# A hybrid decoder layer on one core: FFN up-projection by seven quarter products, with the down-projection as a stage of its own

## The chip, the cores and the metric

One core of one Trainium2 chip runs the whole program. The metric is the device time of one execution in microseconds; three runs of the kernel before and the profile of one execution are given.

## What is computed

A decoder layer for 1024 tokens and 16 meta tokens in front of them (1040 columns; the kernels keep tokens on the free axis and channels on the partitions, in blocks of 128). Two branches, a chunked retention and a differential attention, are projected, mixed by sigmoid gates and added to the residual stream h; a gated MLP with a causal depthwise convolution of width 3 follows. The part around the change:

```python
y   = retention_out @ w_ret_o * sigmoid(gr) + diff_out @ w_diff_o * sigmoid(gd)
h   = x + y @ w_out                                   # (1040, 1024)
u   = rmsnorm(h, norm2_w) @ w_up                      # (1040, 2 * 2816)
u   = causal_dwconv(u, conv_w, conv_b)                # per channel, 3 taps
a, b = split(u)
out = h + (silu(a) * b) @ w_down                      # rows of the meta tokens removed
```

Everything is float32 to the reference's precision.

## The kernel before

Each float32 operand of a product is split into a high and a low fp32r part, and a product is three matmuls, high x high, high x low and low x high (`mm3`, `bulk`). Weights arrive as blocks [128, 8, 128] in two halves of 256 KB (`load_w`, L221); ScalarE casts a half to the high part (L227) and GpSimd subtracts for the low part (L230). A single list, `self.stream`, sets the order of weights, and `next_w` keeps one block ahead; all loads go through SyncE's queue. Activations are split by `split`: a cast on ScalarE (L242) and a subtraction on VectorE or GpSimd (L247). Every matmul is issued by line L175 and has its own weight load.

The program runs in four phases. Phases 1 and 2 are the projections, both attention branches and ret_out, with projection products put between the steps of the attention (`blend`), and with work that waits for other engines put off by some units (`defer`). Phase 3 merges: for each of 8 output blocks of diff_o and of w_out, three column groups of 342 (`QG`), 24 matmuls each. While w_out runs, squares of h are summed (L1025 on ScalarE, L1026 on GpSimd), and h times `norm2_w` is split (`normed`); the row statistics are put off into the first FFN products, and their reciprocal root, spread over the partitions in `rb2`, is multiplied in when the up-projection leaves PSUM (L1079).

Phase 4 loops over 22 channel blocks f. For each, two up products (blocks f and 22 + f), 3 groups of 24 matmuls of 342 columns each; VectorE takes them out of PSUM (L1079), then runs the convolution (`conv`: one TS, L1086, and two STT, L1088, of 1024 columns), ScalarE the Silu (L1124), VectorE the product (L1125), and ScalarE and GpSimd split it. Between the up products stands the down product of an earlier pair of blocks (`down`): 8 output blocks, two halves of 512 columns, 6 matmuls each, added to h in SBUF from PSUM (L1103). h stays in SBUF, and the last down product stores it to the output (L1105).

The order on each engine is the order of the program's calls; the tile framework puts semaphores where an instruction needs another's result or a buffer that another still reads.

## Time and profile before

| | |
|---|---|
| three runs, us | 2614.42, 2614.18, 2611.49; median 2614.18 |
| profiled execution, first to last instruction | 2609.7 us (what lies around it isn't listed) |
| TensorE matmuls | 15444, busy 2520.9 us (97%) |
| VectorE, ScalarE, GpSimd busy | 1667.5, 898.4, 865.4 us |
| first diff_o product to the last matmul's end | 1678.2 to 2606 us |
| granted clock, mean | 0.989 of 2.4 GHz |

Busy times of an engine can hide which stretch is limited by what, so the table is to be read with the stretches below. Times of a matmul in the views are from its start to its modelled end, and overlap; the step from start to start is its price.

### The profile page before, as it was taken

How to read it: one execution, taken by the hardware profiler on the slowest of the kernel's cores; microseconds unless marked ns; L12 is line 12 of the kernel's file. 1: busy time of each engine (PE TensorE's matmuls, PEld its weight loads, DVE VectorE, ACT ScalarE, POOL GpSimd, SP SyncE). 2: the span in 40 equal slices, each digit the busy share in tenths (PEclk: the TensorE clock that was granted, in tenths of full speed). 3: DMA queues.
4: the chain of work that ended last, by engine and by line, in shares of the span. 5: the costliest groups of instructions: out<-in, count | busy, mean ns of one | idle time of the engine just before them, and what ended most of it. 6: DMA issues, size and time to landing. Idle time of an engine off the chain costs nothing.

```text
span 2609.7 us, 40439 instructions
## 1 busy us (share of the span) xinstructions
PE 2520.9 (97%) x15444; PEld 2420.4 (93%) x15444; DVE 1667.5 (64%) x3359; ACT 898.4 (34%) x1903; POOL 865.4 (33%) x644
## 2 busy tenths in 40 slices
PE   7899999999999999999999999999999999999999
PEld 6898999999999999999999898999999999999998
DVE  8687877657474756654677888452376555555555
ACT  3344434344252433433456654332321111111111
POOL 4433343313132222212333333443333333333332
PEclk8999999999999999999999999999999999999999
DMA  4121221222222121223343434523111111111112
GB/s 175 58 78 64 67 79 61 81 87 67 84 64 78 57 87 62 75 83 103 108 115 86 120 88 122 177 98 112 45 48 47 49 49 49 43 47 49 49 49 85
DMA packets 165777, 205.37 MB, mean 79 GB/s; under 512 B 25560, under 2 KB 108112, under 8 KB 165584
## 3 DMA queue, kind: packets, MB, share of 16 engines
q1 hardware_dynamic: 165440, 202.70, 24.4%
q8 instruction: 121, 1.98, 0.3%
q14 instruction: 72, 0.59, 0.1%
q10 hardware_dynamic: 144, 0.10, 0.0%
HBM read 160.20 MB, written 42.35 MB: 78 GB/s over the span
## 4 chain that ended last, share of the span: by engine, by line
PE 76%; DVE 15%; issue 4%; ACT 2%; DMA 2%; SPq 1%; POOL 0%; DVEq 0%; ACTq 0%; POOLq 0%
PE acc L175 43%; PE sc L175 27%; PE ot L175 3%; DVE b L567 3%; PE st L175 2%; DMA b<-d 1%; DVE b L499 1%; ACT b L609 1%; PE sc L625 1%; DVE b L602 1%; DVE al L247 1%; DVE b L501 1%; DVE sql L247 1%; DVE sh L498 1%; DVE b L521 1%
## 5 line engine op out<-in xcount | busy, mean ns | idle before, releaser
L175 PE MATMUL acc<-b,wh 128*128 128x342 f32 (+3 forms) x6076 | 1484.6, 327 | 30.7 <-DVE b L252 6.6
L175 PEld LDWEIGHTS acc<-b,wh 128*128 128x128 f32 x6076 | 1055.1, 190 | 46.3 <-DVE b L253 7.3
L175 PE MATMUL acc<-b,wl 128*128 128x342 f32 (+3 forms) x3038 | 987.2, 325 | 0.3 <-POOL wl L230 0.3
L230 POOL TENSOR_TENSOR wl<-wr,wh 128x512 fp32r<-128x512 f32 x370 | 514.1, 1408 | 1114.2 <-ACT wh L227 1103.8
L175 PE MATMUL sc<-b,wh 128*128 128x342 f32 (+2 forms) x2452 | 616.2, 334 | 0.0
L175 PEld LDWEIGHTS acc<-b,wl 128*128 128x128 f32 x3038 | 577.0, 190 | 5.7 <-POOL wl L230 0.6
L175 PEld LDWEIGHTS sc<-b,wh 128*128 128x128 f32 x2452 | 432.1, 189 | 20.9
L227 ACT CAST wh<-wr 128x512 fp32r<-128x512 f32 x370 | 214.6, 618 | 574.2 <-issue 286.3
L175 PE MATMUL sc<-b,wl 128*128 128x342 f32 (+2 forms) x1226 | 410.6, 335 | 0.8 <-POOL wl L230 0.8
L247 POOL TENSOR_TENSOR b<-b,b 128x512 fp32r<-128x512 f32 (+2 forms) x90 | 147.9, 1644 | 317.2 <-ACT b L242 275.4
L175 PEld LDWEIGHTS sc<-b,wl 128*128 128x128 f32 x1226 | 231.8, 189 | 11.4 <-POOL wl L230 1.3
L242 ACT CAST b<-b 128x512 fp32r<-128x512 f32 (+2 forms) x135 | 99.9, 745 | 233.0 <-DVE b L1125 146.2
L609 ACT ACTIVATE b<-b,sm 128x272 f32<-128x272 f32 (+7 forms) x128 | 100.9, 789 | 227.0 <-DVE sm L608 174.6
L534 DVE TENSOR_TENSOR ev<-acc,b 128x342 f32<-128x342 f32 (+1 forms) x144 | 74.0, 514 | 132.8 <-PE acc L175 115.8
L1088 DVE SCALAR_TENSOR_TENSOR b<-b,cols,b 128x1024 f32<-128x1024 f32 x88 | 148.8, 1691 | 2.3
L602 DVE CUSTOM_DVE_ANT_0 b<-sc,consts 128x144 f32<-128x144 f32 (+6 forms) x224 | 105.9, 503 | 42.7 <-PE sc L175 42.1
L1079 DVE TENSOR_TENSOR b<-sc,b 128x342 f32<-128x342 f32 x84 | 42.5, 511 | 137.3 <-PE sc L175 137.3
L247 DVE TENSOR_TENSOR al<-sc,ah 128x512 fp32r<-128x512 f32 (+2 forms) x144 | 77.5, 539 | 56.8 <-ACT ah L242 55.4
L1103 DVE TENSOR_TENSOR b<-b,sc 128x512 f32<-128x512 f32 x117 | 78.6, 682 | 48.9 <-PE sc L175 48.9
L242 ACT CAST ah<-sc 128x512 fp32r<-128x512 f32 (+2 forms) x144 | 67.3, 468 | 122.3 <-PE sc L625 94.5
L500 POOL TENSOR_TENSOR sh<-sh,b 128x346 f32<-128x346 f32 (+1 forms) x48 | 47.7, 994 | 153.4 <-DVE sh L498 125.5
L567 DVE TENSOR_TENSOR b<-b,b 64x346 fp32r<-64x346 f32 (+1 forms) x96 | 89.4, 931 | 3.7 <-ACT b L566 0.7
(230 smaller groups left out, 2849.6 us busy)
## 6 DMA issues: line engine op xcount, KB each, us to landing
wr<-w_in SPq DMA_DIRECT2D x176, 256.0 KB
wr<-w_up SPq DMA_DIRECT2D x88, 256.0 KB
d<-ev SPq DMA_DIRECT2D x120, 171.0 KB
b<-d SPq DMA_DIRECT2D x256, 64.0 KB
b<-d SPq DMA_DIRECT2D x24, 513.0 KB
wr<-w_down SPq DMA_DIRECT2D x44, 256.0 KB
b<-d SPq DMA_DIRECT2D x32, 260.0 KB
d<-ev SPq DMA_DIRECT2D x48, 173.0 KB
```

What stands on the lines that cost most here:

```text
L175: self.E.matmul(out, lhsT=l, rhs=r, start=start, stop=stop)
L227: self.A.copy(h, raw)
L230: self.G.tensor_sub(l, raw, h.bitcast(F32))
L242: self.A.copy(dh, src)
L247: (self.V if el == "V" else self.G).tensor_sub(dl, src, dh.bitcast(F32))
L500: G.tensor_mul(sh[:, :n], sh[:, :n], self.Sn[:, cs])
L534: V.tensor_mul(o[:, :n], ps[:, :n], self.rb[:, cs])
L567: V.tensor_sub(dst[o, cs], raw[r, cs], dst[r, cs].bitcast(F32))
L602: V.tensor_tensor_reduce(out=sc_[:m, a0:a0 + sz], in0=ps[:m, :sz], in1=mk, scale=1.0, scalar=3e38, op0=ALU.add, op1=ALU.min, accum_out=sm[ ...
L609: A.activation(sc_[:m, :n], sc_[:m, :n], AF.Exp, bias=mx, scale=-1.0, accum_out=sm[:m, 10 + c:11 + c])
L1088: V.scalar_tensor_tensor(out=o[:, q], in0=up[:, NMETA - 2 + i:T - 2 + i], scalar=self.cw(i, fi), in1=o[:, q], op0=ALU.mult, op1=ALU.add)
L1103: self.V.tensor_add(h, h, ps)
```

## The change

Seven products of quarter matrices take the place of eight (Strassen's scheme in Winograd's form). The tokens are cut into two halves of 516 columns (two of them from the meta tokens, for the convolution), the contraction into two halves of 512 channels, and the two weight blocks of f (`w_up[f]` and `w_up[22 + f]`) stand for the two halves of the output. Each product then has 4 contraction blocks x 3 parts x 2 pieces of 258 columns = 24 matmuls (`product`, L991), where the same f had 144 matmuls of 342. The operands on the token side, A, B, E, F, H, G and D, are h times `norm2_w` times the root, or sums and differences of its quarters, made once and kept split (`operand_a` in phase 3 for A and B, `operands_b` behind it for the rest). Those on the weight side are made per f on VectorE from the raw halves (`weight_steps`: s1 = c + d, c + a, a + s1, b + a') and then split by ScalarE and GpSimd, seven halves of 512 per f. The products are summed in PSUM where the scheme allows (A then B; F then H then G; E then D) and taken out through the sums sw, su and two more; ScalarE copies two.

With this go other moves:
- The pools of phases 1 and 2 are closed after ret_out (`back`) and others opened: 5 weight buffers, 3 double PSUM banks, 2 single ones.
- diff_o and w_out run in two column halves of about 516, each in two pieces of 254 to 258; w_out is streamed twice, once for each half, so that the first half's statistics and operands A and B are made while the second half runs. Blocks 0 to 3 have their products A and B in a prologue (`PRO = 4`).
- The convolution's first tap moves from VectorE to ScalarE.
- The finished activations and h go to DRAM; after the 22 blocks, a separate loop loads them back in pairs, splits them (ScalarE and GpSimd) and runs the down products with 512 columns; VectorE adds 1024 columns at a time.

```diff
+    def back(self, ctx):
+        self.flush()
+        self.front.close()
...
+        self.wp = pool("w2", 5)
+        self.tp = pool("tmp2", 2)
+        self.ps = pool("ps2", 3, space=PSUM)
+        self.ahead = 3
+        self.stream = [a["w_diff_o"][i] for i in range(8)] + 2 * [a["w_out"][i] for i in range(8)]
...
+    def product(self, ps, pieces, pairs, start=True, stop=True, more=False):
+        last = len(pairs) - 1
+        for i, ((wh, wl), (xh, xl)) in enumerate(pairs):
+            for l, x, f, e in ((wh, xh, start and i == 0, False), (wh, xl, False, False), (wl, xh, False, stop and i == last)):
+                for g, (t0, n) in enumerate(pieces):
+                    self.E.matmul(ps[:, 512 * g:512 * g + n], lhsT=l, rhs=x[:, t0:t0 + n], start=f, stop=e, skip_group_check=more)
+    PIECES = [(0, 258), (258, 258)]
+    HALF = [[(14, 254), (268, 256)], [(524, 258), (782, 258)]]
...
     def phase3(self):
...
+        for i, pieces in enumerate(self.HALF):
...
+            while m < 8:
+                w = self.next_w()
+                if i and m == 7:
+                    self.first_weights()
+                ps = self.dbl()
+                self.product(ps, pieces, [((w[0][:, k, :], w[1][:, k, :]), x(k)) for k in range(8)])
+                finish(m, i, ps)
+                if i:
+                    S.dma_start(out=self.hs[m], in_=self.h[m][:, NMETA:])
+                    if m == 0:
+                        stat(0)
+                    elif m == 2:
+                        spread(0)
+                    elif m in (3, 4, 5, 6):
+                        for k in (2 * (m - 3), 2 * (m - 3) + 1):
+                            self.operand_a(k)
+                m += 1
+        stat(1)
+        self.prologue(0)
+        spread(1)
+        self.prologue(1)
+        self.operands_b()
...
+    def operand_a(self, k):
+        x = self.xa[k // 2][:, 516 * (k % 2):516 * (k % 2) + 516]
+        self.V.scalar_tensor_tensor(out=x, in0=self.h[k][:, 8:524], scalar=self.n2[k], in1=self.rb2[:, 8:524], op0=ALU.mult, op1=ALU.mult)
+        self.put("A" if k < 4 else "B", k % 4, x, "G")
...
+    def split_w(self, w, raw):
+        self.A.copy(w[0], raw)
+        self.G.tensor_sub(w[1], raw, w[0].bitcast(F32))
...
+    def weight_steps(self, f):
...
+        if not pro:
+            w1 = self.tile_w()
+            q["A"], q["B"] = self.half(w1, 0), self.half(w1, 1)
+            self.split_w(q["A"], ra)
+        yield
...
+        V.tensor_add(s1, rc, rd)
+        V.tensor_add(rc, rc, ra)
+        V.tensor_add(ra, ra, s1)
+        yield
+        self.split_w(q["F"], ra)
+        if not pro:
+            self.split_w(q["B"], rb)
+        yield
...
+        self.split_w(q["H"], rc)
+        V.tensor_add(rb, rb, ra)
...
     def conv(self, fi, up):
-        V = self.V
...
-        V.tensor_scalar(out=o[:, q], in0=up[:, q], scalar1=self.cw(2, fi), scalar2=self.cb(fi), op0=ALU.mult, op1=ALU.add)
+        self.A.activation(o[:, :SEQ], up[:, 8:8 + SEQ], AF.Identity, bias=self.cb(fi), scale=self.cw(2, fi))
...
     def phase4(self):
...
+            first_w()
+            if f >= self.PRO:
+                self.quad_product(pt, f, "B", True)
+                others()
+                A.copy(self.two(ua[:, :516]), self.pair(pt, 258))
+            self.quad_product(pw, f, "H", True)
+            others()
+            V.tensor_sub(self.two(su), self.pair(pw, 258), self.two(st))
...
+        for p in range(NF // 2):
+            gh, gl = down
+            for m in range(8):
...
+                self.product(ps, [(0, 512), (512, 512)], [((w[0][:, o + i, :], w[1][:, o + i, :]), (gh[i], gl[i])) for i in range(2)])
+                V.tensor_add(h[m][:, :SEQ], h[m][:, :SEQ], ps)
+                if p == NF // 2 - 1:
+                    self.S.dma_start(out=self.a["out"][m], in_=h[m][:, :SEQ])
```

Where instructions stand now, at three places. Names begin with their tile's tag: wr a raw weight, wh and wl its parts, d and sc PSUM, b an activation buffer.

VectorE in a steady FFN block, before: three additions out of PSUM, the convolution, and the same for the second block.

```order
L1079 TENSOR_TENSOR b3504_21672<-sc3503_21647,b3341_20345 128x342
L1079 TENSOR_TENSOR b3504_21672<-sc3505_21674,b3341_20345 128x342
L1079 TENSOR_TENSOR b3504_21672<-sc3506_21700,b3341_20345 128x342
L1086 TENSOR_SCALAR b3507_21726<-b3504_21672,cols_92 128x1024
L1088 SCALAR_TENSOR_TENSOR b3507_21726<-b3504_21672,cols_92,b3507_21726 128x1024 x2
L1079 TENSOR_TENSOR b3513_21765<-acc3512_21740,b3341_20345 128x342
L1079 TENSOR_TENSOR b3513_21765<-acc3514_21767,b3341_20345 128x342
L1079 TENSOR_TENSOR b3513_21765<-sc3515_21793,b3341_20345 128x342
L1086 TENSOR_SCALAR b3516_21819<-b3513_21765,cols_92 128x1024
L1088 SCALAR_TENSOR_TENSOR b3516_21819<-b3513_21765,cols_92,b3516_21819 128x1024 x2
L1125 TENSOR_TENSOR b3507_21726<-b3507_21726,b3516_21819 128x1024
```

VectorE in a steady block of the changed kernel. The first row takes the last product, D, out of PSUM; L1323 is sw of the next block.

```order
L1349 TENSOR_TENSOR b3656_23492<-sw3665_23535,d3676_23637 128x516
L1222 TENSOR_TENSOR wr3682_23751<-wr3682_23751,wr3693_23796 128x512
L1231 TENSOR_TENSOR wr3685_23757<-wr3685_23757,wr3682_23751 128x512
L1272 SCALAR_TENSOR_TENSOR b3681_23747<-b3656_23492,cols_95,b3681_23747 128x1024 x2
L1272 SCALAR_TENSOR_TENSOR b3692_23792<-b3667_23537,cols_95,b3692_23792 128x1024
L1323 TENSOR_TENSOR sw3688_23764<-b3679_23721,d3691_23767 128x516
L1272 SCALAR_TENSOR_TENSOR b3692_23792<-b3667_23537,cols_95,b3692_23792 128x1024
L1282 TENSOR_TENSOR b3681_23747<-b3681_23747,b3692_23792 128x1024
L1220 TENSOR_TENSOR wr3716_24025<-wr3706_23982,wr3707_23984 128x512
L1221 TENSOR_TENSOR wr3706_23982<-wr3706_23982,wr3705_23980 128x512
L1340 TENSOR_TENSOR su3689_23765<-d3691_23767,b3679_23721 128x516
```

The PSUM reads fell from six of 342 to five of 516 columns. Four additions of weights (L1220, L1221, L1222, L1231) of later blocks stand among them, and sw stands behind the weight additions and three STT of the block before.

GpSimd at the end of w_out, before: weight splits (L230) and squares (L1026) alternate.

```order
L230 TENSOR_TENSOR wl3319_20223<-wr3320_20224,wh3318_20222 128x512
L230 TENSOR_TENSOR wl3319_20223<-wr3321_20228,wh3318_20222 128x512
L1026 TENSOR_TENSOR b3237_19522<-b3237_19522,sq3317_20219 128x342
L1026 TENSOR_TENSOR b3237_19522<-b3237_19522,sq3324_20260 128x342
L1026 TENSOR_TENSOR b3237_19522<-b3237_19522,sq3326_20289 128x342
L230 TENSOR_TENSOR wl3343_20347<-wr3344_20348,wh3342_20346 128x512
L230 TENSOR_TENSOR wl3343_20347<-wr3345_20352,wh3342_20346 128x512
L1026 TENSOR_TENSOR b3237_19522<-b3237_19522,sq3328_20318 128x342
L230 TENSOR_TENSOR wl3347_20357<-wr3348_20358,wh3346_20356 128x512
L230 TENSOR_TENSOR wl3347_20357<-wr3349_20362,wh3346_20356 128x512
```

GpSimd at the same place of the changed kernel, second half of w_out. L251 splits operands B, L1189 up-projection weights, L1069 adds the squares; the last row adds those of the last block.

```order
L1069 TENSOR_TENSOR b3249_19750<-b3249_19750,sw3340_20619 128x516
L1189 TENSOR_TENSOR wl3364_20788<-wr3361_20783,wh3363_20787 128x512
L1189 TENSOR_TENSOR wl3364_20788<-wr3362_20785,wh3363_20787 128x512
L1069 TENSOR_TENSOR b3249_19750<-b3249_19750,su3346_20689 128x516
L1189 TENSOR_TENSOR wl3368_20798<-wr3365_20793,wh3367_20797 128x512
L251 TENSOR_TENSOR b3348_20695<-b3253_19754,b3347_20694 128x516 x2
L1069 TENSOR_TENSOR b3249_19750<-b3249_19750,sw3352_20753 128x516
L1189 TENSOR_TENSOR wl3368_20798<-wr3366_20795,wh3367_20797 128x512
L251 TENSOR_TENSOR b3350_20697<-b3254_19755,b3349_20696 128x516 x2
L1189 TENSOR_TENSOR wl3415_21192<-wr3409_21182,wh3414_21191 128x512
L1189 TENSOR_TENSOR wl3415_21192<-wr3413_21190,wh3414_21191 128x512
L1069 TENSOR_TENSOR b3249_19750<-b3249_19750,su3370_20853 128x516
```

Between two additions of squares stand splits that the products there don't need yet.

SyncE around the first diff_o weights, before:

```order
L970 DMA b3134_18659<-d1199_7051 128x256 x3
L967 DMA b3137_18670<-d1458_8607 128x1026
L221 DMA wr3100_18428<-w_ret_o 128x512
L221 DMA wr3109_18518<-w_diff_o 128x512
L970 DMA b3138_18671<-d1459_8608 128x258
L970 DMA b3138_18671<-d1459_8608 128x256 x3
L967 DMA b3141_18682<-d1718_10164 128x1026
L970 DMA b3142_18683<-d1719_10165 128x258
```

and in the changed kernel:

```order
L1010 DMA b3141_18700<-d1978_11724 128x1026
L1013 DMA b3142_18701<-d1979_11725 128x258
L1013 DMA b3142_18701<-d1979_11725 128x256 x3
L1023 DMA b3145_18712<-d2159_12818 128x1026
L1023 DMA b3146_18715<-d1972_11664 128x1026
L1023 DMA b3159_18748<-d2184_12968 128x1026
L1023 DMA b3160_18751<-d1995_11791 128x1026
L971 DMA wr3149_18720<-w_diff_o 128x512
L971 DMA wr3150_18724<-w_diff_o 128x512
```

The weight's load stood among the loads of the attention's rows (L967, L970). It now follows all of them and the gates (L1023), and goes to a buffer of the new pool, which opens when the last ret_out product has read the old one.

## Rows read from the trace of the kernel before

**Rows 1.** The page's engine totals (busy us, share of the span, instructions) and its chain that ended last, by engine.

```profile
PE 2520.9 (97%) x15444; PEld 2420.4 (93%) x15444; DVE 1667.5 (64%) x3359; ACT 898.4 (34%) x1903; POOL 865.4 (33%) x644
...
PE 76%; DVE 15%; issue 4%; ACT 2%; DMA 2%; SPq 1%; POOL 0%; DVEq 0%; ACTq 0%; POOLq 0%
```

**Rows 2.** Busy time by stretch: start and end in us, its length, then busy us and instructions (x) of TensorE's matmuls (PE) and weight loads (PEld), VectorE, ScalarE and GpSimd, the granted clock, the DMA share and rate. The last products of ret_out, everything from the first diff_o product on, and the steady FFN blocks.

```profile
1653.60:1678.20 24.60, 24.59 (x156) 24.52 (x157) 10.91 (x16) 7.72 (x10) 10.19 (x7) 1.00 0.39 129
1678.20:2606.00 927.80, 926.42 (x5390) 878.18 (x5388) 510.26 (x562) 184.75 (x267) 322.87 (x213) 1.00 0.18 62
1935.00:2557.00 622.00, 622.00 (x3561) 584.54 (x3560) 365.00 (x387) 102.94 (x148) 202.70 (x130) 1.00 0.15 48
```

**Rows 3.** The chain that ended last, in order of time, merged: start us, us, engine, tile, line and number of instructions. diff_o (1682), the up-projection (1890, 1905), the last down products, and the last addition.

```profile
1682.24 15.12 PE sc L175 x96
...
1890.25 15.06 PE sc L175 x96
1905.31 7.53 PE acc L175 x48
...
2595.94 5.59 PE sc L175 x24
...
2605.75 0.69 DVE b L1103
```

**Rows 4.** The timeline of TensorE in the attention stage: start us, duration us, instruction. The steps from start to start are what counts; the lines left out are the eight other matmuls of 256 columns between 229.00 and 230.07.

```profile
228.76 0.28 PE L175 MATMUL sc<-sqh,constsr 128*128 128x258 f32 x1
228.87 0.29 PE L175 MATMUL sc<-sql,constsr 128*128 128x258 f32 x1
229.00 0.28 PE L175 MATMUL sc<-sqh,constsr 128*128 128x256 f32 x1
...
230.07 0.27 PE L175 MATMUL ot<-ah,vh 128*128 128x128 f32 x1
```

**Rows 5.** Instructions from 1678 to 2606 us by line and shape: count (x), busy us, mean ns of one, then the engine's idle time before them and what ended it.

```profile
L230 POOL TENSOR_TENSOR wl<-wr,wh 128x512 fp32r<-128x512 f32 x162 | 231.4, 1450 | 436.1 <-ACT wh L227 436.1
L1088 DVE SCALAR_TENSOR_TENSOR b<-b,cols,b 128x1024 f32<-128x1024 f32 x88 | 148.8, 1691 | 2.3
...
L227 ACT CAST wh<-wr 128x512 fp32r<-128x512 f32 x162 | 92.7, 618 | 379.9 <-issue 191.9 <-PE sc L175 108.8 <-PE acc L175 75.7
...
L1086 DVE TENSOR_SCALAR b<-b,cols 128x1024 f32<-128x1024 f32 x44 | 82.2, 1868 | 1.6
L1103 DVE TENSOR_TENSOR b<-b,sc 128x512 f32<-128x512 f32 x117 | 78.6, 682 | 48.9 <-PE sc L175 48.9
...
L1125 DVE TENSOR_TENSOR b<-b,b 128x1024 f32<-128x1024 f32 x22 | 26.8, 1219 | 1.3
L1124 ACT ACTIVATE b<-b 128x1024 f32<-128x1024 f32 x22 | 23.3, 1061 | 108.1 <-DVE b L1088 108.1
```

**Rows 6.** Two stretches of the timeline of VectorE (DVE) and GpSimd (POOL) in the FFN, and behind them the durations of line L1088 (min/median/max in ns).

```profile
2303.06 1.87 DVE L1086 TENSOR_SCALAR b<-b,cols 128x1024 f32<-128x1024 f32 x1
2303.09 3.00 POOL L230 TENSOR_TENSOR wl<-wr,wh 128x512 fp32r<-128x512 f32 x2 [8.82 <-ACT wh L227]
...
2304.96 3.53 DVE L1088 SCALAR_TENSOR_TENSOR b<-b,cols,b 128x1024 f32<-128x1024 f32 x2
...
2566.40 1.27 DVE L1088 SCALAR_TENSOR_TENSOR b<-b,cols,b 128x1024 f32<-128x1024 f32 x1
...
2570.53 1.27 DVE L1103 TENSOR_TENSOR b<-b,acc 128x512 f32<-128x512 f32 x2
2570.57 2.42 POOL L247 TENSOR_TENSOR b<-b,b 128x1024 fp32r<-128x1024 f32 x1 [5.77 <-ACT b L242]
...
2572.95 2.54 POOL L230 TENSOR_TENSOR wl<-wr,wh 128x512 fp32r<-128x512 f32 x2
...
L1088 DVE SCALAR_TENSOR_TENSOR b<-b,cols,b x88: 1267/1712/2207, 1888.6 to 2566.4; 128x1024 f32<-128x1024 f32 x88
```

**Rows 7.** Busy time by stretch, columns as in rows 2, around two pauses of TensorE: near the start, and ahead of the last ret_out products.

```profile
81.30:86.30 5.00, 0.26 (x3) 0.01 (x1) 2.22 (x3) 1.45 (x4) 0.00 (x0) 0.90 0.59 141
86.30:93.10 6.80, 6.70 (x24) 6.41 (x24) 6.45 (x7) 6.57 (x14) 5.99 (x5) 0.57 0.24 80
1650.20:1653.60 3.40, 0.33 (x3) 0.05 (x1) 1.75 (x3) 0.43 (x1) 0.00 (x0) 1.00 0.70 251
1653.60:1660.00 6.40, 6.39 (x40) 6.39 (x41) 3.17 (x4) 1.76 (x3) 4.92 (x3) 1.00 0.12 43
```

**Rows 8.** The timeline of loads and of what waited for them: the first diff_o weight, the last head's rows, and the first weights of the kernel (SPq is the queue that issues them).

```profile
1644.31 0.33 SPq L221 DMA_DIRECT2D wr<-w_diff_o  x1
...
1647.06 3.14 SPq L970 DMA_DIRECT2D b<-d  x4
1651.85 1.29 DVE L971 SCALAR_TENSOR_TENSOR b<-b,qkw,b 128x1026 f32<-128x1026 f32 x1 [4.53 <-DMA b<-d]
...
1.18 0.89 SPq L221 DMA_DIRECT2D wr<-w_in  x2
...
5.83 0.62 ACT L227 CAST wh<-wr 128x512 fp32r<-128x512 f32 x1 [3.16 <-DMA wr<-w_in]
```

More of the change, by code (lines that the diff above doesn't have):

```diff
@@ L210, in next_w @@
     def next_w(self):
-        while len(self.loaded) < 2 and self.stream:
+        while len(self.loaded) < self.ahead and self.stream:
             self.loaded.append(self.load_w(self.stream.pop(0)))
@@ L746, in phase1 @@
         seq += fill[7 * DH:]
[L747 to L752 removed]
         self.loaded = []
[L754 to L755 removed]
+        self.stream = [a["w_in"][b] for _, _, b in seq] + [a["w_ret_o"][i] for i in range(16)]
         self.norm_in()
@@ new lines, in phase3 @@
+            ml.append(self.big(F32R))
+            for pieces in self.HALF:
+                ps = self.dbl()
+                cs = slice(pieces[0][0], sum(pieces[1]))
+                self.product(ps, pieces, [((w[0][:, k, :], w[1][:, k, :]), (dh[k], dl[k])) for k in range(8)])
+                for o, p, _ in self.evacuated(gd, ps, pieces):
+                    V.tensor_mul(o, p, o)
+                V.tensor_add(mx[:, cs], mx[:, cs], gd[:, cs])
+                if m == 7:
+                    self.split(mh[m][:, cs], ml[m][:, cs], mx[:, cs])
@@ new lines, in phase3, with finish @@
+            if m < 7:
+                self.split(mh[m][:, q], ml[m][:, q], mx[:, q], el="V")
+        self.h = []
+        for m in range(8):
+            h = self.big()
+            S.dma_start(out=h[:, 8:], in_=self.a["xT"][m][:, 8:])
+            self.h.append(h)
+        self.hs = [self.dram([P, SEQ]) for _ in range(8)]
+        sq, self.rb2 = self.big(), self.big()
+        self.xa = [self.big() for _ in range(4)]
+        self.ops = {}
+        def finish(m, i, ps):
+            for o, p, _ in self.evacuated(self.h[m], ps, self.HALF[i]):
+                V.tensor_add(o, p, o)
+            hs = slice(8 + 516 * i, 524 + 516 * i)
@@ new lines, in finish, with stat @@
+                A.activation(x, self.h[m][:, hs], AF.Square)
+                G.tensor_add(sq[:, hs], sq[:, hs], x)
+        y = []
+        def stat(i):
+            hs = slice(8 + 516 * i, 524 + 516 * i)
+            s = self.big(F32R)
+            self.split(s[:, :516], s[:, 516:1032], sq[:, hs])
+            st = self.sng()
+            for j in range(2):
+                self.stat(st[:, :258], self.S4[j], [s[:, 258 * j + 516 * k:258 * j + 258 + 516 * k] for k in range(2)], j == 0, j == 1)
+            r, rr = self.big(), self.big(F32R)
+            x, yy, t = (r[:, 258 * j:258 * j + 258] for j in range(3))
+            V.tensor_scalar(out=x, in0=st[:, :258], scalar1=1.0 / 8, scalar2=EPS, op0=ALU.mult, op1=ALU.add)
+            self.rsqrt(yy, x, t)
+            self.split(rr[:, :258], rr[:, 258:516], yy, scale=1 / RS)
+            y[:] = [rr[:, :258], rr[:, 258:516]]
@@ new lines, in phase3, with operand, put, xs @@
+        stat(1)
[3 more added lines that the diff above has]
+        self.operands_b()
+    PRO = 4
+    def operand(self, name):
+        if name not in self.ops:
+            self.ops[name] = [(self.big(F32R), self.big(F32R)) for _ in range(2)]
+        return self.ops[name]
+    def put(self, name, k, x, el="V"):
+        h, l = self.operand(name)[k // 2]
+        c = slice(516 * (k % 2), 516 * (k % 2) + 516)
+        self.split(h[:, c], l[:, c], x, el=el)
+    def xs(self, name, k):
+        c = slice(516 * (k % 2), 516 * (k % 2) + 516)
+        return [t[:, c] for t in self.ops[name][k // 2]]
@@ new lines, in quad_product, with temp, two, prologue @@
+    def quad_product(self, ps, f, name, more=False):
+        w = self.wq[f].pop(name)
+        self.product(ps, self.PIECES, [((w[0][:, k, :], w[1][:, k, :]), self.xs(name, k)) for k in range(4)], not more, True, more)
+    def temp(self, tag, bufs):
+        return self.tp.tile([P, 516], F32, tag=tag, name=self.nm(tag), bufs=bufs)
+    @staticmethod
+    def two(t): return t.rearrange("p (a b) -> p a b", a=2)
+    def prologue(self, part):
+        if part == 0:
+            self.pro = {}
+        new = []
+        for f in (2 * part, 2 * part + 1):
+            ps, ua = self.dbl(), self.work()
+            self.quad_product(ps, f, "A")
+            self.A.copy(self.two(ua[:, 516:1032]), self.pair(ps, 258))
+            self.pro[f] = ua
+            new.append(ps)
+        for f, ps in zip((2 * part, 2 * part + 1), new):
+            self.quad_product(ps, f, "B", True)
+            self.A.copy(self.two(self.pro[f][:, :516]), self.pair(ps, 258))
@@ L1090, in conv @@
[L1090 to L1105 removed]
+            self.V.scalar_tensor_tensor(out=o[:, :SEQ], in0=up[:, 6 + i:6 + i + SEQ], scalar=self.cw(i, fi), in1=o[:, :SEQ],
+                                        op0=ALU.mult, op1=ALU.add)
@@ L1137, in hybrid_layer, with down_load @@
+    def down_load(self, p):
+        gh, gl = [], []
+        for i in range(2):
+            x = self.big()
+            self.S.dma_start(out=x[:, :SEQ], in_=self.acts[2 * p + i])
+            gh.append(self.big(F32R)[:, :SEQ])
+            gl.append(self.big(F32R)[:, :SEQ])
+            self.split(gh[i], gl[i], x[:, :SEQ], el="G")
+        return gh, gl
 @with_exitstack
@@ L1140, in hybrid_layer @@
     b.phase2(*b.phase1())
+    b.back(ctx)
     b.phase3()
```

314 lines of the change are left out of this document (181 added, 133 removed).

## Prediction

> **What bounds the kernel now.** I read the page's engine totals and chain first. TensorE is busy 97% of the span, and the chain that ended last is 76% TensorE [rows 1]. A share of the whole span hides where the slack is, so next came the busy time by stretch [rows 2]: from the last products of ret_out (1653.60 us) to the end, TensorE has no idle time worth naming (926.42 busy of 927.80 us from the first diff_o product on), while VectorE, ScalarE and GpSimd are busy 510, 185 and 323 us of it. The chain there is one run of TensorE pieces [rows 3]. In the second half of this kernel, therefore, a TensorE microsecond saved is a microsecond saved, and a TensorE wait added is a microsecond lost. Everything the change does lies in this half. The program of the phases before 1678 us keeps its matmuls and their order, so I put it at no change.
>
> A matmul's price must be read from start to start, because the durations of overlapping matmuls are longer than their share. The chain gives it by division [rows 3]: 48 matmuls of 342 columns in 7.53 us and 96 in 15.06 are 0.157 us each (0.1575 in diff_o); 24 of 512 columns in 5.59 are 0.233. For narrow ones the timeline of the attention stage serves [rows 4]: nine steps of 256 columns from 229.00 to 230.07 are 0.119 each, and two of 258 from 228.76 to 229.00 are 0.120.
>
> **The change on TensorE.** Before, the up-projection is 22 x 2 blocks x 3 groups x 24 = 3168 matmuls x 0.1569 = 497.1 us. After, it is 22 x 7 products x 24 = 3696 matmuls of 258 columns x 0.120 = 443.5. That is **-53.6**: an eighth of the columns goes (62), but narrower matmuls give 8 back. diff_o and w_out go from 1152 x 0.1573 = 181.2 to 1536 x 0.1195 = 183.6: **+2.4**. The down products stay 1056 of 512 columns. Sum on TensorE: **-51.2**. The uncertain price is 258 columns: 0.119 by the nearest row; 0.130 is the largest single step in rows 4, which would give back 37 us. I take the mean of the two 258 steps.
>
> **What it adds, in order of the program.**
>
> *The seam at 1678 us.* Before, the first diff_o weight is asked for at 1644.31 [rows 8], 34 us ahead. Now its buffer belongs to a pool that opens where the old one closed, so the load waits for the last ret_out product. Then come the transfer, a ScalarE cast of 0.62 and a GpSimd subtraction of 1.27 [rows 5, 6]. The transfer is bounded by two rows [rows 8]: 1.65 us from the end of the last issue before 1651.85 to the work that needed it (a smaller load), and 4.65 from 1.18 to 5.83 in the crowded start. I take 2.2, since the seam is nearer the first: **+4.2** with the hand-overs, bounds 3.6 to 6.6. All of it is TensorE idle.
>
> *The end of w_out's second half.* The statistics product stat(1) stands in TensorE's order inside prologue products A of blocks 0 and 1. It needs the last addition of squares, which GpSimd reaches only behind 23 operations that became possible when the first half's statistics were spread: 8 operand splits, 8 weight splits, 2 of block 0's, 5 additions. That is 23 x 1.27 = 29.2, with 1.3 to start and 1.3 for the split behind it 31.8, against 264 matmuls x 0.12 = 31.7 of cover. What decides is how GpSimd shares with VectorE. Rows 6 show it: the STT at 2304.96 met a running subtraction that ended at 2306.09, and the two STT took 3.53 where the one at 2566.40, alone, took 1.27: the first waited. VectorE's additions with a PSUM input ran beside GpSimd at 2570.53 undisturbed (0.64 each). In this stretch VectorE issues 16 two-input SBUF operations of about 0.69 (half of the 1024-wide 1.27 and 1.22, as L1103's 0.68 is for 512 [rows 5]), 11.0 us. None colliding gives 0.1, all 11; half gives **+5.6**.
>
> *Operands of the second half.* 44 VectorE operations of 516 columns x 0.69 = 30.4 us build E, F, H, G and D behind spread(1). The first Winograd sum sw of block 0 stands behind all 44 in VectorE's order, and product H of block 0 may not start before it: 31.1 us plus 1.0 for the statistics' copy, against cover from prologue(1), E and F of 144 x 0.12 = 17.3. **Uncovered: 14.8.** Seven GpSimd splits (8.9) fall into it; a third of them in the way makes it **+18**, all of them +24. Then blocks 1 to 4 have only five products each, 14.4 us, for 12.5 us of VectorE work (next part) that collides with five splits; half of these (3.2) in the way makes 15.7: 4 x 1.3 = **+5.2** (bounds 0 and 18).
>
> *The steady block.* VectorE per block: 5 PSUM sums x 0.69, 4 weight sums x 0.69, 4 STT x 1.27, a product 1.22 = 12.5 us; GpSimd 7 x 1.27 = 8.9; ScalarE seven casts of 0.62, three passes of 1.06 and two copies, below 9; TensorE 168 x 0.12 = 20.2. On totals TensorE still bounds. The order decides: from the end of D the freed weight buffer lets ScalarE cast (0.62), GpSimd split A and B (2.54), VectorE add (0.69), run three STT (3.81) and then sw (0.69); with five hand-overs 8.6 us, against A, F and B, 72 x 0.12 = 8.64. Slack is nil, so each collision in it counts. One holds up to 1.27; half of one per block: 17 x 0.6 = **+10.2** (0 to 22). If the cover were gone, the next to be late is G, behind the sum su.
>
> *The end.* TensorE meets the down weights, split by GpSimd, after the last block, and the last addition (0.69, rows 3) becomes one of 1024 columns and its store doubles: **+6.5**, of which 1.4 is sure; 10 at most.
>
> *The clock.* After 5.00 us of idling at 81.30 the granted clock was 0.57 for 6.80 us, i.e. 1.2 GHz for most of it; after 3.40 us at 1650.20 it stayed 1.00 [rows 7]. At half rate 6.80 us loses about 3. Stalls of 5 and more are expected in two places, and the seam (4.2) lies between the two rows: 2 x 3.1 + 1.5 = **+7.7** (0 to 12).
>
> Sum: -51.2 + 4.2 + 5.6 + 18 + 5.2 + 10.2 + 6.5 + 7.7 = **+6.2**. Against the profiled span 2609.7 that is 2615.9; the median of the runs stands 4.5 above this span (the lowest 1.8), so **2620**.
>
> The Trainium skill, page "SBUF — State Buffer", section "Who interferes with whom", says that a VectorE operation with two SBUF inputs and a GpSimd operation that reads SBUF exclude each other for the whole instruction. By that rule the trace agrees: L1088's 2207 ns against 1267, and L1103 unmoved at 0.68 [rows 5, 6]. Priced without it, the collisions above (5.5, 3.2, 5.2, 10.2) fall away and the sum would be -18, or 2596; with it, it is the +6.2. The same rule spares the five PSUM sums, so that 9.1 + 8.9 = 18.0 of 20.2 us per block are exclusive.
>
> **The rivals.**
> 1. *The waits overlap better: faster.* If VectorE's and GpSimd's operations interleave so that collisions delay nothing TensorE waits for, only the uncovered parts stay: -51.2 + 4.2 + 0.1 + 14.8 + 1.4 and one clock drop of 3.1 = -27.6, **2587**. For it: on totals the engines have 8 us of slack per block. Against: rows 6 show each meeting to cost what is left of the other's operation, and the chain at each block's start has no slack. It decides where the wait of H in a block is under 0.3 us.
> 2. *The two engines run as one: slower still.* If VectorE and GpSimd hardly overlap at all, a block takes 12.5 + 8.9 = 21.4 us instead of 20.2: 17 x 1.2 = 20.4 for 10.2, with all collisions in the earlier parts (11, 24, 18): +41, **2655**. For it: each hand-over behind a blocked operation passes the delay on, 1868 ns for L1086, which takes half the inputs [rows 5]. Against: L1103 ran beside GpSimd unmoved.
> 3. *The narrow matmuls don't save.* At 0.1345 us a matmul of 258 columns the 3696 cost the old 497. Then the change does nothing of what it says, and only its waits remain: +60, 2674. Against: nine steps of 0.119 in rows 4. For it: those are short runs among others, not 168 in a row.
>
> **How the numbers follow.** Forecast 0.48, rival 1 0.33, rival 2 0.15, rival 3 0.04. A measurement of this kernel tells about 0.2% (5.2 us) from no change, so "same" is 2609 to 2619.4. The forecast lies at its edge: its own spread (2603 to 2640) gives 0.05 faster, 0.12 same, 0.31 slower. With rival 1 split 0.31 faster and 0.02 same, this makes faster 0.36, same 0.14, slower 0.50. The range holds the forecast, rival 1 and the lower half of rival 2: **2584 to 2650**; the likeliest case's own is 2603 to 2640.
>
> **What would show it.** In the profile of the changed kernel: matmuls of 258 columns 0.120 apart; TensorE idle of some 4 us at 1678, 5 to 6 before the statistics of the second half, 18 before product H of block 0, about 0.6 in each later block with VectorE sw as releaser; the granted clock below 1 after the long ones; STT of 1024 above 1.27 where GpSimd runs. Steps of 0.13 would sink the first term. TensorE without idle in the steady blocks would make rival 1 right; waits of more than 1.2 us per block, rival 2. A changed time ahead of 1678 us would be something I haven't seen.

## The result, and the profile after

The changed kernel takes 2638.0 us (median of 4, 2637.6 to 2638.5) where the kernel before takes 2614.3 in the same session: a ratio of 1.0089, 95% interval 1.0075 to 1.0103. It is slower by 24 us; forecast were 2620, slower, and a range of 2584 to 2650. The profiled execution took 2637.8 us for a span of 2636.0. The same 1.8 lies around the span of before (2611.49 for 2609.7), so of the 4.5 that I put on the span, 2.7 was the spread of the runs.

The totals of the page, to be held against [rows 1]: TensorE has 916 matmuls more and is busy 21 us less, and the span is 26 longer.

```profile
PE 2500.1 (95%) x16360; PEld 2389.3 (91%) x16360; DVE 1700.0 (64%) x3341; ACT 1026.7 (39%) x2089; POOL 998.8 (38%) x727
```

Busy time by stretch, columns as in [rows 2]: the seam, diff_o and w_out up to the second half's statistics, the wait for these, the prologue with E and F of block 0, the wait of product H of block 0, blocks 0 to 4, blocks 5 to 20, the last block, the down stage.

```profile
1679.20:1684.50 5.30, 0.19 (x2) 0.00 (x0) 0.51 (x1) 2.62 (x3) 2.35 (x1) 0.82 0.95 291
1684.50:1874.50 190.00, 189.79 (x1567) 189.42 (x1567) 76.62 (x96) 68.98 (x106) 115.19 (x80) 0.99 0.46 158
1874.50:1884.00 9.50, 0.27 (x3) 0.06 (x2) 3.55 (x3) 0.62 (x1) 8.75 (x7) 0.64 0.32 112
1884.00:1921.10 37.10, 33.68 (x248) 33.06 (x249) 30.05 (x45) 16.47 (x32) 11.10 (x8) 0.91 0.13 43
1921.10:1929.50 8.40, 0.30 (x4) 0.12 (x2) 8.40 (x15) 4.52 (x9) 8.40 (x1) 0.73 0.00 1
1929.50:2007.00 77.50, 66.73 (x487) 65.69 (x488) 55.15 (x55) 27.94 (x36) 27.37 (x21) 0.90 0.20 65
2007.00:2346.00 339.00, 331.13 (x2683) 324.44 (x2682) 240.88 (x225) 134.19 (x190) 165.23 (x112) 1.00 0.23 75
2346.00:2389.00 43.00, 40.78 (x301) 38.61 (x300) 23.10 (x21) 18.60 (x26) 27.48 (x17) 1.00 0.50 163
2389.00:2636.00 247.00, 239.92 (x1021) 192.64 (x1020) 108.36 (x89) 39.40 (x54) 90.98 (x54) 0.99 0.29 102
```

Length less PE busy is TensorE's idle in each; some 0.17 us of each wait stay hidden, because durations overlap. Before, the one row 1678.20 to 2606.00 [rows 2] had 1.4 us of it, at a clock of 1.00. Now every stretch but the second has some, and the granted clock is 0.64 to 0.91 at the seam and from the statistics to block 4.

Who was waited for, TensorE alone, from 1678 us (total us, times, longest):

```profile
PE d L991 <- DVE sw L1323: 19.5, 6, 8.1
PE s L179 <- ACT b L246: 9.2, 1, 9.2
PE d L991 <- DVE su L1340: 7.6, 17, 0.9
PE d L991 <- ACT wh L231: 5.1, 1, 5.1
PE d L991 <- DVE b L1371: 2.1, 1, 2.1
```

The first wait is sw, the Winograd sum that the prediction named, but its six are blocks 0 to 4 and the last; in the steady blocks the one that stands out is su (17 times). (There sw holds up the weight load ahead of the matmul, which this list of matmuls leaves out.)

A steady block is best read on VectorE and GpSimd together. First VectorE: start us, duration us, instruction.

```profile
2196.59 0.68 DVE L1323 TENSOR_TENSOR sw<-b,d 128x516 f32<-128x516 f32 x1
...
2198.58 2.13 DVE L1282 TENSOR_TENSOR b<-b,b 128x1024 f32<-128x1024 f32 x1
2200.63 1.78 DVE L1220 TENSOR_TENSOR wr<-wr,wr 128x512 f32<-128x512 f32 x1
...
2203.06 0.69 DVE L1340 TENSOR_TENSOR su<-d,b 128x516 f32<-128x516 f32 x1
...
2211.67 1.76 DVE L1222 TENSOR_TENSOR wr<-wr,wr 128x512 f32<-128x512 f32 x1 [1.10 <-POOL wl L1189]
...
2217.83 0.68 DVE L1323 TENSOR_TENSOR sw<-b,d 128x516 f32<-128x516 f32 x1
```

GpSimd in the same time:

```profile
2197.80 4.06 POOL L1189 TENSOR_TENSOR wl<-wr,wh 128x512 fp32r<-128x512 f32 x2 [6.17 <-ACT wh L1188]
...
2210.34 2.54 POOL L1189 TENSOR_TENSOR wl<-wr,wh 128x512 fp32r<-128x512 f32 x2 [1.56 <-ACT wh L1188]
```

From sw (2196.59) to the next sw (2217.83) are 21.24 us; 168 matmuls at 0.1206 (below) are 20.26. The product L1282 takes 2.13 instead of 1.22 and the weight sum L1220 1.78 instead of 0.69, both while GpSimd's pair of splits runs (4.06 us for two that take 2.54 at 2210.34). That is 2.0 us lost on VectorE ahead of su, which then ends too late for product G, 0.6 us after TensorE was ready. L1222 has waited 1.10 for GpSimd's split and takes 1.76, and sw is late behind it. The other five of GpSimd's seven splits take their own 1.27 us each.

**The order.** The words ahead of the prediction say that the order on each engine is that of the calls. That is not exact: the tile framework moves instructions within their dependences, as the sw between two STT in the order shown there tells, and as experiment 6 met.

### The profile page after: what moved, and what is told of

Same layout as the page of the kernel before. It is cut to its first block, busy times and chain, and to the rows that moved or that the text cites. A ratio compares the mean times of both kernels' runs of the same rounds, so it can differ in the third digit from the quotient of the medians.

```text
span 2636.0 us, 42975 instructions
## 1 busy us (share of the span) xinstructions
PE 2500.1 (95%) x16360; PEld 2389.3 (91%) x16360; DVE 1700.0 (64%) x3341; ACT 1026.7 (39%) x2089; POOL 998.8 (38%) x727
## 5 line engine op out<-in xcount | busy, mean ns | idle before, releaser
L179 PE MATMUL acc<-b,wh 128*128 128x342 f32 (+2 forms) x4880 | 1188.7, 326 | 27.4 <-ACT wh L231 6.1
L179 PEld LDWEIGHTS acc<-b,wh 128*128 128x128 f32 x4880 | 848.0, 191 | 32.0 <-ACT wh L231 6.1
L991 PE MATMUL d<-b,wh 128*128 128x258 f32 (+2 forms) x4192 | 767.8, 305 | 39.7 <-DVE sw L1323 19.5
L179 PE MATMUL acc<-b,wl 128*128 128x342 f32 (+2 forms) x2440 | 789.1, 323 | 0.0
L234 POOL TENSOR_TENSOR wl<-wr,wh 128x512 fp32r<-128x512 f32 x298 | 403.5, 1372 | 788.5 <-ACT wh L231 746.5
L991 PEld LDWEIGHTS d<-b,wh 128*128 128x128 f32 x4192 | 620.4, 192 | 81.7 <-issue 14.8
L991 PE MATMUL d<-b,wl 128*128 128x258 f32 (+3 forms) x2096 | 466.6, 304 | 0.2 <-POOL wl L234 0.2
L991 PEld LDWEIGHTS d<-b,wl 128*128 128x128 f32 x2096 | 341.4, 192 | 16.4 <-POOL wl L234 0.5
L1189 POOL TENSOR_TENSOR wl<-wr,wh 128x512 fp32r<-128x512 f32 x154 | 234.0, 1537 | 253.7 <-ACT wh L1188 251.4
L251 POOL TENSOR_TENSOR b<-b,b 128x512 fp32r<-128x512 f32 (+3 forms) x98 | 159.2, 1629 | 238.4 <-ACT b L246 212.8
L246 ACT CAST b<-b 128x512 fp32r<-128x512 f32 (+4 forms) x165 | 116.8, 717 | 197.5 <-DMA b<-d 73.2
L246 ACT CAST ah<-sc 128x512 fp32r<-128x512 f32 (+2 forms) x144 | 67.3, 468 | 122.9 <-PE sc L629 94.1
L251 DVE TENSOR_TENSOR al<-sc,ah 128x512 fp32r<-128x512 f32 (+2 forms) x144 | 77.6, 539 | 57.5 <-ACT ah L246 56.1
```

Source lines behind the costliest of these rows:

```text
L179: self.E.matmul(out, lhsT=l, rhs=r, start=start, stop=stop)
L234: self.G.tensor_sub(l, raw, h.bitcast(F32))
L246: self.A.copy(dh, src)
L251: (self.V if el == "V" else self.G).tensor_sub(dl, src, dh.bitcast(F32))
L991: self.E.matmul(ps[:, 512 * g:512 * g + n], lhsT=l, rhs=x[:, t0:t0 + n], start=f, stop=e, skip_group_check=more)
L1189: self.G.tensor_sub(w[1], raw, w[0].bitcast(F32))
```

## The experiments

My theory: TensorE's work fell about as forecast, and was eaten by waits, (a) because GpSimd and VectorE's operations with two SBUF inputs hold each other up, and GpSimd's split is a slow link, (b) in the stages where VectorE's or GpSimd's queue is longer than TensorE's cover, and (c) because pauses bring slow-clock stretches. The main rival: VectorE simply has too much to do. All experiments start from the changed kernel (2638.0); "before" took 2615.5 and 2614.5 in their sessions.

### 1. The seam: two weights loaded ahead

```diff
         self.ret_tail()
+        self.early = [self.early_w(self.a["w_diff_o"][i]) for i in range(2)]
         for _ in prev:
...
+    def early_w(self, blk):
+        t = lambda d: self.big(d)[:, :8 * P].rearrange("p (a b) -> p a b", a=8)
+        w, raw = (t(F32R), t(F32R)), t(F32)
...
-        self.stream = [a["w_diff_o"][i] for i in range(8)] + 2 * [a["w_out"][i] for i in range(8)]
+        self.loaded = self.early
+        self.stream = [a["w_diff_o"][i] for i in range(2, 8)] + 2 * [a["w_out"][i] for i in range(8)]
```

> The first two diff_o weights are loaded and split into activation buffers while ret_out still runs, so that they don't wait for the old pools to close. If the 5.3 us of TensorE idle at 1679 us is the load's wait, it shrinks to 2 us or less and the slow-clock stretch behind it (granted clock 0.67 over 7.5 us) goes too: 3 to 6 us in all, time 2632 to 2635. Rival: the seam is held by the PSUM banks of the old pool or by the loads of the gates that stand ahead in the queue; then the idle stays above 4 us and the time at 2637 to 2639.

Measured 2636.5 us (2633.8 to 2639.4), ratio to before 1.0085 [1.0071, 1.0099]. The first product now starts 1.0 us after the last of ret_out, but 5 us later TensorE waits 3.3 and 2.1 us for the last head's operand: the loads of that head's rows need buffers that the early weights hold. Late rows also hold VectorE ahead of the last ret_out products, where TensorE now waits 2.5 us. Neither theory had this: the wait only moved. Experiment 8 tries with fewer buffers.

### 2. Squares on VectorE

```diff
-                G.tensor_add(sq[:, hs], sq[:, hs], x)
+                (V if i else G).tensor_add(sq[:, hs], sq[:, hs], x)
```

> In w_out's second half VectorE instead of GpSimd adds the squares of h. Theory: the 9.4 us of TensorE idle before the second half's statistics are GpSimd's queue of splits, so the idle falls to 5 us or less (the operand splits still stand there), and the time by 4 to 8 us to 2630 to 2634. Rival: the idle is the chain of ScalarE's square, the split and the statistics behind the last product itself, on whichever engine; then it stays near 9 us and the time at 2637 to 2639.

Measured 2633.0 us (2630.2 to 2633.8), 1.007 [1.0056, 1.0084]. In the changed kernel ScalarE's last square (1872.81) waits for GpSimd until 1881.53, behind splits:

```profile
1872.81 0.63 ACT L1068 ACTIVATE su<-b 128x516 f32<-128x516 f32 x1
...
1879.09 2.48 POOL L1189 TENSOR_TENSOR wl<-wr,wh 128x512 fp32r<-128x512 f32 x2
...
1881.53 1.72 POOL L1069 TENSOR_TENSOR b<-b,su 128x516 f32<-128x516 f32 x1
```

With the addition on VectorE:

```profile
1876.67 1.73 DVE L1220 TENSOR_TENSOR wr<-wr,wr 128x512 f32<-128x512 f32 x1 [4.30 <-POOL wl L1189]
1878.33 0.68 DVE L1069 TENSOR_TENSOR b<-b,su 128x516 f32<-128x516 f32 x1
...
1879.72 0.58 PE L179 MATMUL s<-b,constsr 128*128 128x258 f32 x1 [5.66 <-ACT b L246]
```

The time came into the theory's range; the wait falls from 9.2 to 5.7 us, not to 5 or less: VectorE's queue holds L1220, a weight sum, ahead of the addition, and L1220 had waited 4.30 us for a GpSimd split. VectorE, taking its queue in order here, handed on its own wait.

### 3. Eight splits to an idle GpSimd

```diff
-        self.split(h[:, c], l[:, c], x, el=el)
+        self.split(h[:, c], l[:, c], x, el="G" if name in "GD" else el)
```

> The 12 low-part subtractions... of operands H's successors G and D, 8 of them, go from VectorE to GpSimd, which is idle there for two thirds of the time. Theory (the two engines exclude each other while VectorE reads two SBUF inputs): GpSimd's 1.3 us each takes more than the 0.69 us that VectorE saves, the wait of product H of block 0 (8.3 us) shrinks by no more than 4 and what follows grows; time 2635 to 2640. Rival (VectorE's amount of work alone decides): 8 x 0.69 = 5.5 us less ahead of sw, all of it off that wait; time 2630 to 2633.

Measured 2634.3 us (2631.3 to 2636.0), 1.0074 [1.0061, 1.0087], between the two expectations. The wait of H fell from 8.3 to 5.5 us, half of the 5.5 that VectorE no longer had to do, and the one behind it grew (su 0.9 to 1.4). VectorE's splits from 1884 to 1932 us: count, busy us, mean ns. In the changed kernel

```profile
L251 DVE TENSOR_TENSOR b<-b,b 128x516 fp32r<-128x516 f32 x21 | 14.5, 736 | 0.4 <-ACT b L246 0.3
```

and here

```profile
L251 DVE TENSOR_TENSOR b<-b,b 128x516 fp32r<-128x516 f32 x13 | 11.8, 937 | 0.4 <-ACT b L246 0.3
```

With five splits more on GpSimd there (1715 ns each in the mean, where about 1.3 us is their own time), VectorE's rose from 736 to 937 ns, for about 690 of their own. So meetings give back half of what the smaller number of VectorE operations saves.

GpSimd's weight splits in this stretch take 2499 ns in the mean in the changed kernel, but that is one operation of eight: seven take 1.3 to 1.7 us, and one 9.62. The same operation in experiment 2, whose kernel has the same work there, took 1.62:

```profile
1920.26 9.62 POOL L1189 TENSOR_TENSOR wl<-wr,wh 128x512 fp32r<-128x512 f32 x1 [7.29 <-ACT wh L1188]
```

```profile
1915.94 1.62 POOL L1189 TENSOR_TENSOR wl<-wr,wh 128x512 fp32r<-128x512 f32 x1 [7.41 <-ACT wh L1188]
```

The long one stood while VectorE ran fourteen two-input operations without a pause, and ended 1.2 us after VectorE came to sw, which reads PSUM. H waited for sw and not for it.

### 4. Weight splits on VectorE

```diff
     def split_w(self, w, raw):
         self.A.copy(w[0], raw)
-        self.G.tensor_sub(w[1], raw, w[0].bitcast(F32))
+        self.V.tensor_sub(w[1], raw, w[0].bitcast(F32))
```

> The low-part subtractions of the up-projection's weights (seven of 512 columns per block) go from GpSimd to VectorE, which then has some 17.3 us of work in a block of 21.2. Theory (meetings of GpSimd with two-input VectorE operations, and GpSimd's longer 1.3 us in each chain, make the waits): the idle in the steady blocks falls from 0.8 to under 0.3 us a block, that before blocks 1 to 4 from 10.5 to under 5, that before the statistics from 9.4 to under 5; in all 20 to 30 us less idle, time 2605 to 2620. Rival (TensorE waits for VectorE because VectorE has too much to do): 4.8 us more VectorE work in each block make the waits longer, by 1 to 3 us a block; time 2655 to 2690.

Measured 2594.9 us (2591.5 to 2595.9), ratio to before 0.9924 [0.9911, 0.9936]: 43 us faster than the changed kernel, more than the theory's range, and the rival is out. Steady blocks, busy time by stretch, first the changed kernel, then this one:

```profile
2010.00:2330.00 320.00, 312.58 (x2533) 306.30 (x2533) 227.96 (x213) 127.19 (x180) 156.39 (x105) 1.00 0.23 76
```

```profile
2010.00:2330.00 320.00, 320.00 (x2656) 320.00 (x2655) 247.11 (x323) 135.64 (x191) 7.36 (x4) 1.00 0.24 83
```

VectorE has done 108 splits more, and its other work for 15.8 blocks instead of 15.1, and is busy only 19 us more; 108 x 0.684 alone would be 74. The rest it no longer loses to GpSimd. TensorE has no idle left. Its waits from 1678 us:

```profile
PE d L991 <- DVE sw L1323: 10.8, 1, 10.8
...
PE s L179 <- ACT b L246: 2.6, 1, 2.6
```

What is left of sw is block 0 alone; su is gone. Two sums sw of this kernel stand at

```profile
2205.14 0.68 DVE L1323 TENSOR_TENSOR sw<-b,d 128x516 f32<-128x516 f32 x1
...
2225.40 0.68 DVE L1323 TENSOR_TENSOR sw<-b,d 128x516 f32<-128x516 f32 x1
```

20.26 us apart: the price of 168 matmuls without a wait, 0.1206 each. The prediction's 0.120 was right.

### 5. GpSimd in the way, with nobody reading its result

```diff
         self.V.tensor_sub(w[1], raw, w[0].bitcast(F32))
+        idle = self.tp.tile([P, 4, 112], F32, tag="idle", name=self.nm("idle"), bufs=1)
+        part = w[0].bitcast(F32)[:, :, :112]
+        self.G.tensor_sub(idle, part, part)
```

> As the kernel with the weight splits on VectorE (2594.9 us), and GpSimd again runs a subtraction for each of them, on the high part (448 of 512 columns, about 1.14 us), into a scratch tile that nobody reads, so nothing waits for GpSimd. Theory (GpSimd and VectorE's two-input operations exclude each other): VectorE's operations get longer (STT of 1024 above 1.4 us in the mean) and most of the 43 us are lost again, time 2615 to 2650. Rival (GpSimd's splits were only too slow a link of the chains): nothing hangs on them now, so time 2592 to 2598 and VectorE's durations unchanged.

Measured 2615.0 us (median of 11, 2612.9 to 2620.3), ratio to before 1.0005 [0.9996, 1.0014], at the lower edge of the theory's range: 20 of the 43 us are lost again to work whose result nothing reads, where the theory had most of them. The same stretch as above, and VectorE's and GpSimd's groups in it:

```profile
2010.00:2330.00 320.00, 319.75 (x2621) 316.60 (x2620) 305.42 (x327) 133.82 (x189) 124.27 (x109) 1.00 0.21 76
```

```profile
L1192 POOL TENSOR_TENSOR idle<-wh 128x448 f32<-128x448 f32 x109 | 125.7, 1153 | 195.8 <-ACT wh L1188 192.1
L1189 DVE TENSOR_TENSOR wl<-wr,wh 128x512 fp32r<-128x512 f32 x108 | 119.1, 1136 | 0.0
...
L1285 DVE TENSOR_TENSOR b<-b,b 128x1024 f32<-128x1024 f32 x16 | 30.5, 1906 | 1.7
```

VectorE is busy 305 us for 247 with the same work: splits 1136 ns for 684 at best, the product 1906 for 1226. STT didn't lengthen (1273), against what I had written; in a steady block they stand where GpSimd is still. The block grew from 20.26 to 20.54 us, and the rest of the 20 us lies in blocks 1 to 3, ahead of the statistics (8.5 us of wait for 2.7) and in the slow clock behind these. So meetings are worth some 20 us in this kernel, slow clock included. For the changed kernel that is neither a lower nor an upper bound: the scratch work is a little shorter than the true one, but VectorE has seven splits more per block to be met. Nor is GpSimd quite without followers; from 1860 to 2345 us ScalarE's casts waited for a weight buffer that the scratch subtraction still read:

```profile
ACT wh L1188 <- POOL idle L1192: 35.9, 17, 3.3
```

That is 2.0 us in a steady block, where the same cast stood idle 1.74 in experiment 4. The other 23 us are left for the split as a link that others wait for (1.27 us and its own delays on GpSimd, 0.69 on VectorE); no run measured that part by itself. The Trainium skill, page "SBUF — State Buffer", section "Who interferes with whom", adds that issue order decides who blocks. The trace agrees in so far as VectorE loses where GpSimd's pair is already running (L1282 begins at 2198.58, the pair at 2197.80), and GpSimd where VectorE's run came first (9.62 us in experiment 3); why that operation was held through fourteen of VectorE's, and for so little in experiment 2, no run shows.

### 6. Filler ahead of three waits

```diff
...
+            if f < 4 and f != 2:
+                self.filler({0: 60, 1: 28, 3: 20}[f])
             self.quad_product(pw, f, "H", True)
```

> The changed kernel with matmuls whose result nobody reads (258 columns, operands at hand) put in TensorE's order ahead of product H of blocks 0, 1 and 3: 60, 28 and 20 of them, 7.2, 3.4 and 2.4 us at full clock, about the waits there (8.3, 4.0, 3.1). Theory (a wait costs itself and a slow-clock stretch behind it): no granted clock below 0.9 behind these three waits, 3 to 6 us less, time 2631 to 2635. Rival (behind the waits VectorE's chain is late by the same amount in any case, so that a faster TensorE only waits more): the idle elsewhere grows by what the clock gives, time 2637 to 2640.

`filler(n)` issues n matmuls into a PSUM tile that nothing reads. Measured 2636.8 us (2633.8 to 2640.7), 1.0083 [1.0069, 1.0097]: not to be told from the changed kernel; the median lies at the rival's edge, but the runs spread over both expectations. The framework put most of the filler where operands were ready, so only the wait of block 0 was filled; the 48 matmuls of blocks 1 and 3 (5.8 us at 0.12) were mostly work added. Behind the filled wait the clock did stay up (at 2.4 GHz; a mean of 0.5 or 0.6 below is mostly 1.2 GHz). The changed kernel, behind its wait of 8.1 us, and this one in the same place and behind the next wait, which stayed:

```profile
1929.50:1936.50 7.00, 6.12 (x29) 5.86 (x30) 4.38 (x6) 0.00 (x0) 0.37 (x1) 0.59 0.12 37
```

```profile
1929.00:1936.00 7.00, 7.00 (x58) 6.90 (x58) 4.59 (x7) 0.00 (x0) 0.00 (x0) 1.00 0.00 0
1945.60:1952.00 6.40, 6.34 (x30) 6.34 (x31) 5.57 (x6) 3.55 (x4) 0.00 (x0) 0.52 0.01 3
```

So filling this pause removed the slow stretch behind it. Not every pause has one: behind the wait of 2.6 us ahead of block 3, which stayed as well, the granted clock was 1.00. What the filling is worth here is left open by the times.

### 7. Combined

Experiments 2 and 4, D's splits on GpSimd, the operands G and D made behind sw of block 0, and one early weight (as in 8).

```diff
...
+        def rest():
+            for k in range(4):
+                V.tensor_sub(xa(4 + k), xa(4 + k), xa(k))
+                self.put("G", k, xa(4 + k))
+            for k in range(4):
+                self.put("D", k, sl(xd, k))
+        self.rest = rest
...
+            if f == 0:
+                self.rest()
             if f >= self.PRO:
                 self.quad_product(pt, f, "B", True)
```

> Weight splits and squares of w_out's second half on VectorE, operand D's splits on GpSimd, operands G and D made behind the sum sw of block 0, and the first diff_o weight (one block, two activation buffers) loaded ahead of the seam. If the waits add up as the separate kernels show: from 2594.9 the wait of H of block 0 (11 us) falls to 5 to 6, the one before the statistics (2.8) to 1.5, the seam (5.7) to 2 to 5: 8 to 11 us less, with one slow-clock stretch fewer, time 2583 to 2589. Rival: VectorE now sets the pace there, so each shortened wait comes back at the next product; time 2592 to 2597.

Measured 2588.4 us (2587.4 to 2591.6), ratio to before 0.9900 [0.9885, 0.9915]; it beats both kernels, and 6.5 of the 8 to 11 us came. TensorE's waits:

```profile
PE d L997 <- ACT b L246: 4.8, 3, 2.4
...
PE d L997 <- DVE sw L1332: 2.5, 1, 2.5
PE s L179 <- ACT b L246: 1.7, 1, 1.7
```

The wait of H of block 0 fell from 10.8 to 2.3 us, and that for the statistics to 1.7. It is one of the three behind ACT b L246 above, and its line is

```profile
1908.43 1.20 PE L997 MATMUL d<-b,wh 128*128 128x258 f32 x4 [2.25 <-ACT b L246]
```

The 2.5 behind sw are a new wait, of H of block 1, so a part of the gain came back there. The seam's waits stayed (next).

### 8. The seam with one weight

```diff
+    def early_w(self, blk):
+        t = lambda: self.big(F32R)[:, :8 * P].rearrange("p (a b) -> p a b", a=8)
+        return self.load_w(blk, (t(), t()))
```

> Only one diff_o weight loaded ahead, into two activation buffers and the old pool's raw buffers, where the earlier try took six activation buffers and the loads of the last head's rows came 9 us later for want of them. If that shortage was what ate the gain, the last rows are in time now: idle at the seam under 2.5 us, time 2632 to 2635. If the weight's transfer shares the queue with rows that are late anyhow, idle of 4 us and more stays, 2636 to 2640.

Measured 2636.3 us (2635.4 to 2638.1), 1.0081 [1.0067, 1.0094], in the rival's range; idle at the seam 0.8 + 2.7 + 2.2 = 5.7 us. The timeline of experiment 7, which has the same seam, shows what is late there:

```profile
1678.49 1.75 SPq L1019 DMA_DIRECT2D b<-d  x4
1680.34 2.97 SPq L977 DMA_DIRECT2D wr<-w_diff_o  x6
...
1685.78 1.29 DVE L1020 SCALAR_TENSOR_TENSOR b<-b,qkw,b 128x1026 f32<-128x1026 f32 x1 [5.20 <-DMA b<-d]
...
1688.20 0.50 PE L997 MATMUL d<-b,b 128*128 128x254 f32 x2 [2.35 <-ACT b L246]
```

The last head's rows (L1016, L1019) are scaled at 1685.78, when their load lands; in the changed kernel that was done at 1666.66, before the seam. Two things make them late. The two buffers taken still put their issue off: L1016 is issued at 1676.16, when an earlier head's rows have been scaled (1674.85 + 1.28), for 1654.09 in the changed kernel. And they land 5.5 us after the end of their issue (1680.24), with six weight loads issued right behind them, where 1.65 did before [rows 8]; that is nearer to the rival's reason. Which of the two decides isn't shown. Loading ahead without taking a buffer wasn't tried.

## Why the prediction held, and where it was off

Slower, for the reason given, within the range; the forecast itself was 18 us low. By its own terms, in us from the first diff_o product on:

| term | forecast | measured | from |
|---|---|---|---|
| TensorE's work | -51.2 | -49 | 3696 x 0.1206 = 445.7 for 497.1; and 190.0 - 2.5 of slow clock for 1568 matmuls to 1874.5, or 183.6 for the 1536 of diff_o and w_out, for 181.2 |
| seam | 4.2 | 5.1 | first row of the stretches |
| statistics | 5.6 | 9.2 | waits |
| operands, blocks 0 to 4 | 18 + 5.2 | 12 + 11 | 3.4 + 8.1, and 10.8, and what overlap hides |
| steady blocks and the last | 10.2 | 18 | 16 x (21.25 - 20.26) + 2.5 |
| end | 6.5 | 4 | a wait of 2.1, small ones of 0.6, and 0.9 from the last product to the end |
| slow clock | 7.7 | 14 | below |

That sums to 24; 1.0 more came ahead of the seam, and the spans differ by 26.

- **The matmul price held.** 0.120 from two steps of 258 columns became 0.1206 over whole blocks. Rival 3, that narrow matmuls don't save, is out.
- **The places of the waits held**: the seam, the statistics, H of block 0, the steady blocks.
- **That the operands came out at 23 is luck.** Product H of block 0 and the products ahead of it waited 12 us where I had 18, and blocks 1 to 4 waited 11 where I had 5.2: two errors of 6 us that cancel.
- **The steady block was mis-sized.** I took half a meeting, 0.6 us, in the chain to sw. Meetings cost 2 us on VectorE ahead of su and another 1.1 ahead of sw, and the block lost 1.0. I had called G behind su the next to be late; it was the first. In experiment 5, where the engines meet as well but no result of GpSimd is waited for, a block lost 0.28; so most of the 1.0 seems to need the split as a link too.
- **The statistics were mis-sized**, and not in the meetings. From 1844 to the last addition of squares GpSimd's 25 operations take 4.8 us more than their own 1.29 each, near the 5.5 that I took. What I had at nothing is a wait inside GpSimd's queue: it stands idle for 2.75 us, for a square of h that comes late, because the addition to h stands on VectorE behind weight sums, the first of which waits 5.71 us for a GpSimd split:

```profile
1861.05 1.77 DVE L1220 TENSOR_TENSOR wr<-wr,wr 128x512 f32<-128x512 f32 x1 [5.71 <-POOL wl L1189]
...
1864.55 1.67 DVE L1222 TENSOR_TENSOR wr<-wr,wr 128x512 f32<-128x512 f32 x1
...
1868.43 1.56 POOL L1069 TENSOR_TENSOR b<-b,su 128x516 f32<-128x516 f32 x1 [2.75 <-ACT su L1068]
```

With the forecast's own 0.1 us that leaves 1.5 of the 9.2 open.

- **The clock term had too few pauses.** I counted two and a half, by the row at 5.00 us of idle. In the changed kernel the clock was low behind pauses of 5.1, 9.2, 8.1 and 4.0 us, and also of 2.2 to 3.1 in blocks 2, 3 and at the down stage, whereas before it stayed at 1.00 behind 3.40 [rows 7]. The steps from matmul to matmul that take 1.35 to 2.6 times their usual price (at half clock it is 2) exceed this price by 17 us in all in this kernel, 3 of them short waits in the steady blocks, and by 0.7 in the kernel before.
- **Rival 2**, the two engines nearly in turn, comes near the steady block's time (21.25 us for its 21.4), but five of the seven splits run undisturbed there; and it doesn't fit the stages ahead of it: its 53 us there (11, 24, 18) were 32 (9.2 and 23).
- **Rival 1 described another kernel.** Experiment 4 is the case in which the waits overlap: 2595, between its 2587 and the 2596 that the prediction gives without collisions. It takes GpSimd out of the way, not a luckier interleaving.
